# A two-layer decoder trunk on one core: the first head pair's weights made ahead of the first head's chain, and low parts moved behind the last one

## The chip, the cores and the metric

The kernel runs on one core of a Trainium2 chip. The metric is device time in microseconds (us) of one execution. A core has TensorE (PE, matmuls), VectorE (DVE), ScalarE (ACT), GpSimd (POOL) and SyncE (SP, which issues most DMAs), each with its own queue of instructions in program order; they wait for each other by semaphores.

## The reference

Two layers on a sequence of 1024 rows of width 1024, all in float32. The change touches the first layer's mixer, its output projection, and the start of its FFN.

```
def hgrn2_mixer(h, w_in, lower_bound, g_norm_w, w_out):
    q, f, i, g = jnp.split(h @ w_in, 4, axis=-1)          # 8 heads of 128 each
    fg = lb + (1.0 - lb) * jax.nn.sigmoid(heads(f))
    o = hgrn2_chunkwise(jax.nn.silu(heads(q)), 1.0 - fg, heads(i), jnp.log(fg))
    o = o * lax.rsqrt(jnp.mean(jnp.square(o), -1, keepdims=True) + RMS_EPS)
    o = o * g_norm_w * jax.nn.silu(heads(g))
    return o.reshape(B, S, D) @ w_out
...
h = layer_norm(ALPHA * h + mix, ln_mix_g[0], ln_mix_b[0])
ff = conv_ffn(h, ...)              # up-projection, causal conv of width 3, silu(a) * b, down-projection
h = layer_norm(ALPHA * h + ff, ...)
# then the shared K and V, and a layer with windowed attention and another FFN
```

hgrn2_chunkwise is a gated linear recurrence: a state of 128x128 per head that decays by fg and takes up k and v; in chunks it is a product of decayed scores, plus the carried state.

## The kernel before

**Precision.** Every large matmul is three: an operand is split into a high part (a cast on ScalarE to fp32r, line L249, L1285 or L868) and a low part (source minus high part, helper low_part, L197, on VectorE or POOL), and hi*hi, hi*lo and lo*hi are added in PSUM (helper mm3, lines L222, L223 and L224). T holds x transposed and split; HL is a ring of split weight blocks; raw0 to raw2 are the landing places of loaded weights (rx in the FFN), each loaded again when its last reader is done.

**Projections of the heads.** The weights of head pairs are multiplied by a scheme of seven products on block sums (Strassen's). Its products are numbered 1 to 7; a line of (pair m, product p) is worked through in order. Block sums of x stand in Y0, Y1 and a part of T: xf and xs are the sources, s1 is the tile VG of the "minus first" head, and sums_of_x and last_sums make them (L845 to L848, L868). Block sums of weights are the jobs "a" and "b" (L1305 to L1309): on POOL for pair 0, on VectorE for later ones. job_next makes a sum or a low part, cast_next a cast.

**The chain of a head (recur).** After fg, qs and kp of a head are there, VectorE runs products of decays in levels: L1116 to L1124 form the first, then update(1) to update(6), each L1105, L1107, L1110; between them TensorE makes scores into psax (L228), which masked copies (L1048, L1069) put into Ab and A. update(3) of the first head waits for kd scores. At the end stand the state's products (VG,kd and VG,A) and L1194, L1196. Each head's values and gates lie in VG (L750 to L759), its output is scaled by a square root from POOL (ss, L1223 and L1224) into og.

**What sets the order.** The part up to the first output rows stands in manual_schedule: each engine's order is the order of the code. Generators are stepped by an object od that keeps a modelled time for TensorE (od.t) and VectorE (od.v); a step says when it may come (od.behind), and od.fill is called in the gaps to lay weight jobs. So a cost in the code (od.vec) moves instructions. Outside manual_schedule the framework's scheduler sets the order of all engines.

**The tail.** After the last product, finished heads' outputs come back from memory (hod, L1440) and are split into T (move); out_split splits the four weight blocks of hgrn_w_out. out_pass (L1508) multiplies them for the first four blocks of 128 rows, with the last head missing; when that is done, out_part adds it, L380 adds the residual, and L263 to L283 are the LayerNorm, whose scale and shift are loaded as HL and rx (L414, L415). ffn's class Up takes rows transposed (L232), and its first product reads TX, the block sums of split rows; tiles of pool hp must be done with where TX is placed over them.

```
        VG = {-1: hp.tile([P, 2, S], F32, name="VG", bufs=2)}
        VG[0] = hp.tile([P, 2, S], F32, name="VG", bufs=2)
        ...
        with tc.manual_schedule(engines={EN.PE, EN.SP, EN.Activation, EN.DVE, EN.Pool}):
            pair_load(0, 0)
            od.fill, od.hook, od.room = lay, hook, 0.5
            first_qf(w0)
            pair_load(0, 1)
```

## Time and profile before

| | |
|---|---|
| time, three runs | 2133.52 us median (2132.39 to 2134.44) |
| profiled execution | 2132.9 us, span 2131.1 us |
| granted TensorE clock, mean | 0.996 |
| busy | TensorE 2093.3 us (98%), VectorE 1777.7 us (83%), ScalarE 968.5 us (45%), POOL 205.1 us (10%) |
| DMA | 286.81 MB, mean 135 GB/s |

A row of the timeline is: start in us, duration, engine, line, operation, output<-inputs, shape and count, and in brackets the idle time before it and who ended it. A row of the waits is: engine, tile and line that waited, for whom, then total us, times, and the longest. A row of a stretch of the span is: from:to, length, then busy us and instructions of PE, PEld (weight loads), DVE, ACT and POOL, the granted clock, the share of DMA and its GB/s. Lines after the change are a few higher: L1116 becomes L1125, L1105 becomes L1114, L1048 becomes L1057, L1305 becomes L1315 and so on.

### The profile page before, as it was taken

Reading aid. Unit: us, or ns where it says so; the run is one execution under the profiler, and the core shown is the slowest. Engines: PE = TensorE matmul, PEld = TensorE weight load, DVE = VectorE, ACT = ScalarE, POOL = GpSimd, SP = SyncE. Lnnn points to the kernel's source line nnn. Section 1 sums busy time; section 2 is a strip of 40 time slices with the busy share of each in tenths; the row PEclk is TensorE's granted clock in tenths of the full one; section 3 lists DMA queues with packets and bytes.
Section 4 is the critical chain, followed back from the end, with each engine's and each line's share of the span. In section 5 each row is a group of like instructions: output and inputs, shape, how many; then the busy total and the mean of one; then the engine's idle time right before and its main releaser. Section 6 shows DMA issues by size and latency. Waiting matters only on the chain. (4 is left out here: it accounts for less than half of the span.)

```text
span 2131.1 us, 31572 instructions
## 1 busy us (share of the span) xinstructions
PE 2093.3 (98%) x12303; PEld 1743.4 (82%) x12303; DVE 1777.7 (83%) x2408; ACT 968.5 (45%) x1562; POOL 205.1 (10%) x226
## 2 busy tenths in 40 slices
PE   9899999998999999999999999999999999999998
PEld 8688888887878888888888888888888888888886
DVE  6777777758999998887987758969999999978976
ACT  6455555542444444444433356743544444444430
POOL 2200000000110000100001113321010000000002
PEclk9999999999999999999999999999999999999999
DMA  4011111153238666627854511042266776449662
GB/s 152 21 51 52 54 59 57 55 179 99 89 101 196 160 168 160 164 97 260 300 185 157 172 26 46 23 149 89 81 172 173 176 170 156 129 146 332 224 206 99
DMA packets 239822, 286.81 MB, mean 135 GB/s; under 512 B 30216, under 2 KB 160440, under 8 KB 239416
## 3 DMA queue, kind: packets, MB, share of 16 engines
q1 hardware_dynamic: 223360, 238.26, 34.4%
q0 software_dynamic: 15456, 46.16, 10.9%
q8 instruction: 97, 1.59, 0.3%
q10 hardware_dynamic: 856, 0.37, 0.1%
q14 instruction: 53, 0.43, 0.1%
HBM read 241.72 MB, written 89.15 MB: 155 GB/s over the span
## 5 line engine op out<-in xcount | busy, mean ns | idle before, releaser
L222 PE MATMUL psmm<-T,HL 128*128 128x512 f32 x768 | 303.4, 395 | 0.7 <-ACT qs L1364 0.7
L224 PE MATMUL psmm<-T,HL 128*128 128x512 f32 x768 | 299.6, 390 | 3.0 <-DVE HL L197 3.0
L223 PE MATMUL psmm<-T,HL 128*128 128x512 f32 x768 | 299.1, 390 | 0.9 <-DVE T L197 0.9
L527 DVE SCALAR_TENSOR_TENSOR Y<-Y,cwt,Y 128x1023 f32<-128x1023 f32 (+1 forms) x176 | 225.3, 1282 | 49.0 <-ACT Y L525 47.5
L249 ACT CAST HL<-rx 128x1024 fp32r<-128x1024 f32 (+1 forms) x151 | 151.1, 1007 | 163.7 <-DMA rx<-in_ffn_w_in_dram 32.2
L197 DVE TENSOR_TENSOR HL<-rx,HL 128x1024 fp32r<-128x1024 f32 (+1 forms) x151 | 176.6, 1176 | 18.6 <-ACT HL L249 18.3
L224 PEld LDWEIGHTS psmm<-T,HL 128*128 128x128 f32 x768 | 144.2, 188 | 34.2 <-DVE HL L197 3.9
L223 PEld LDWEIGHTS psmm<-T,HL 128*128 128x128 f32 x768 | 144.4, 188 | 30.0 <-DVE T L197 1.3
L222 PEld LDWEIGHTS psmm<-T,HL 128*128 128x128 f32 x768 | 144.1, 188 | 30.1 <-ACT qs L1364 1.1
L525 ACT ACTIVATE Y<-Y,cwt 128x1024 f32<-128x1024 f32 x88 | 108.8, 1237 | 93.3 <-DVE Y L514 82.8
L222 PE MATMUL psax<-T,HL 128*128 128x512 f32 x352 | 137.3, 390 | 0.0
L224 PE MATMUL psax<-T,HL 128*128 128x512 f32 x352 | 137.0, 389 | 0.0
L223 PE MATMUL psax<-T,HL 128*128 128x512 f32 x352 | 136.9, 389 | 0.0
L197 DVE TENSOR_TENSOR HL<-raw,HL 128x512 fp32r<-128x512 f32 (+1 forms) x121 | 93.7, 798 | 45.7 <-ACT HL L1285 35.9
L271 POOL TENSOR_TENSOR rs<-rs,nhalf 128x1 f32<-128x1 f32 x32 | 45.0, 1406 | 738.1 <-DVE rs L270 738.1
L249 ACT CAST HT<-rx 128x1024 fp32r<-128x1024 f32 (+1 forms) x37 | 35.5, 960 | 135.9 <-DVE rx L481 62.9
L222 PE MATMUL psmm<-HL 128*128 128x512 f32 x220 | 86.8, 395 | 5.4 <-ACT qs L1364 5.4
L224 PE MATMUL psmm<-HL 128*128 128x512 f32 x220 | 86.2, 392 | 0.0
L223 PE MATMUL psmm<-HL 128*128 128x512 f32 x220 | 86.1, 391 | 0.0
L249 ACT CAST HL<-Y 128x1024 fp32r<-128x1024 f32 (+1 forms) x32 | 28.6, 894 | 109.3 <-DVE Y L481 44.5
L222 PEld LDWEIGHTS psax<-T,HL 128*128 128x128 f32 x352 | 66.2, 188 | 13.7
L224 PEld LDWEIGHTS psax<-T,HL 128*128 128x128 f32 x352 | 66.0, 188 | 13.7
(397 smaller groups left out, 5414.3 us busy)
## 6 DMA issues: line engine op xcount, KB each, us to landing
rx<-in_ffn_w_in_dram SPq DMA_DIRECT2D x136, 256.0 KB
rx<-gd SPq DMA_DIRECT2D x118, 256.0 KB
bsd<-in_ffn_w_out_dram POOLq DMA_DIRECT2D x36, 768.0 KB, 8.3
gd<-Y SPq DMA_DIRECT2D x44, 512.0 KB
raw<-in_hgrn_w_in_dram SPq DMA_DIRECT2D x30, 512.0 KB
rx<-in_ffn_w_out_dram SPq DMA_DIRECT2D x54, 256.0 KB
R<-bsd SPq DMA_DIRECT2D x44, 256.0 KB
Y<-in_ffn_w_in_dram SPq DMA_DIRECT2D x40, 256.0 KB
```

Source lines behind the costliest of these rows:

```text
L197: make = lambda e: e.tensor_tensor(lo, src, hi.bitcast(F32), op=ALU.subtract)
L222: nc.tensor.matmul(ps, st(0), mv(0), start=start, stop=False, skip_group_check=onto)
L223: nc.tensor.matmul(ps, st(0), mv(1), start=False, stop=False, skip_group_check=onto)
L224: nc.tensor.matmul(ps, st(1), mv(0), start=False, stop=stop, skip_group_check=onto)
L249: nc.scalar.copy(hi, src)
L271: nc.gpsimd.tensor_tensor(rs, rs, nhalf, op=ALU.pow)
L525: nc.scalar.activation(c, u, AF.Identity, bias=cwt[:, l, 3, ci:ci + 1], scale=cwt[:, l, 2, ci:ci + 1])
L527: nc.vector.scalar_tensor_tensor(c[:, sh:], u[:, :S - sh], cwt[:, l, 2 - sh, ci:ci + 1], c[:, sh:], op0=ALU.mult, op1=ALU.add)
```

## The change

Five things change. The first pair's second weights are loaded earlier in the program, and ensure(1) and ensure(3) force four of its blocks ahead of the first head's chain. The pair's sums and the low parts of x's last sums go from POOL to VectorE, the latter by a step that is placed by od.behind. VG has two named places with og between them, and Up's TX becomes TX and T2. Low parts of the output weights and of moved heads become lists (out_lows, moved_lows) that lay takes, the second only after the last head's update(6). The output passes run hi by hi for all four row blocks first. And manual_schedule ends ahead of the last out_part.

```diff
-            self.TX = pool.tile([P, 3, 2, 4, 512], F32R, name="TX")
+            self.TX = pool.tile([P, 2, 2, 4, 512], F32R, name="TX")
+            self.T2 = pool.tile([P, 2, 4, 512], F32R, name="T2")
...
-        for name, copies in (("fg", 1), ("qs", 1), ("kp", 2), ("kd", 1), ("tot", 1), ("St", 1), ("qp", 1), ("A", 1), ("og", 1)):
+        for name, copies in (("fg", 1), ("qs", 1), ("kp", 2), ("kd", 1), ("tot", 1), ("St", 1), ("qp", 1), ("A", 1)):
             hp.tile([P, S], F32, name=name, bufs=copies)
-        VG = {-1: hp.tile([P, 2, S], F32, name="VG", bufs=2)}
-        VG[0] = hp.tile([P, 2, S], F32, name="VG", bufs=2)
+        def values_and_gates(h):
+            return hp.tile([P, 2, S], F32, name=f"VG{h % 2}")
+        VG = {0: values_and_gates(0)}
+        hp.tile([P, S], F32, name="og")
+        VG[-1] = values_and_gates(-1)
...
                 nc.scalar.copy(t[:, 0], src)
-                low_part(t[:, 1], src, t[:, 0], nc.gpsimd)
-                yield 0.8
+                yield od.behind(0.0, 1.0)
+                low_part(t[:, 1], src, t[:, 0], None)
+                od.vec(0.7)
+                yield 0.1
...
                 proj_T(weights["f"], half, ps)
+                opened[0] = 2 * half
...
             update(6)
+            if h == NH - 1:
+                through.append(1)
...
-                make = nc.vector.tensor_tensor if m else nc.gpsimd.tensor_tensor
                 if p == "a":
-                    make(b12, b22, b12, op=sub)
-                    make(b11, b12, b11, op=add)
+                    tt(b12, b22, b12, op=sub)
+                    tt(b11, b12, b11, op=add)
...
-        later_dve = []
+        out_lows, moved_lows, through = [], [], []
         def lay():
-            if later_dve and later_dve[0][0] <= od.t:
-                later_dve.pop(0)[1]()
+            if job_next():
                 return True
-            return job_next()
+            lows = out_lows or (moved_lows if through else [])
+            if lows and lows[0][0] <= od.t:
+                lows.pop(0)[1]()
+                return True
+            return False
...
             pair_load(0, 0)
+            pair_load(0, 1)
             od.fill, od.hook, od.room = lay, hook, 0.5
             first_qf(w0)
-            pair_load(0, 1)
             pair_load(1, 0)
+            ensure(1)
             opened[0] = 4
             od.finish(fourth)
+            ensure(3)
...
             for tb in range(4):
                 begun.append(psmm())
                 out_pass(begun[tb], tb, 0, 0, range(KC - 2), start=True)
+            lay_all(out_lows)
+            for tb in range(4):
                 out_pass(begun[tb], tb, 0, 1, range(KC - 2))
             od.finish(moved)
             for tb in range(4):
                 out_pass(begun[tb], tb, 0, 0, [KC - 2])
                 out_pass(begun[tb], tb, 0, 1, [KC - 2])
+            lay_all(moved_lows)
+            for tb in range(4):
                 out_pass(begun[tb], tb, 1, 0, range(KC - 1))
...
-            od.fill = od.hook = None
+        od.fill = od.hook = None
...
```

**Where it moves instructions.** On VectorE at the start, between the last low parts of x's sums (Y_309 is Y0) and the first operation of the first head's chain, L1116 (St<-qs,kp). Before:

```order
L197 TENSOR_TENSOR Y_309<-kp,Y_309 128x4x128
L197 TENSOR_TENSOR HL<-kd,HL 128x4x128
L197 TENSOR_TENSOR Y_309<-kd,Y_309 128x4x128
L1116 TENSOR_TENSOR St<-qs,kp 128x1024
L1117 TENSOR_TENSOR qp<-qs,fg 128x1024
```

After, where Y_463 is Y1, raw_113 and raw_114 are the landing places raw1 and raw2, and the chain begins at L1125:

```order
L197 TENSOR_TENSOR Y_309<-kd,Y_309 128x4x128
L197 TENSOR_TENSOR Y_463<-St,Y_463 128x4x128
L197 TENSOR_TENSOR HL<-raw_113,HL 128x512
L1315 TENSOR_TENSOR raw_114<-raw_114 128x512
L1316 TENSOR_TENSOR raw_113<-raw_114,raw_113 128x512
L197 TENSOR_TENSOR Y_463<-qp,Y_463 128x4x128
L197 TENSOR_TENSOR HL<-raw_113,HL 128x512
L197 TENSOR_TENSOR Y_463<-tot,Y_463 128x4x128
L197 TENSOR_TENSOR Y_463<-og,Y_463 128x4x128
L197 TENSOR_TENSOR HL<-raw_113,HL 128x512
L1318 TENSOR_TENSOR raw_113<-raw_113 128x512
L1319 TENSOR_TENSOR raw_113<-raw_114,raw_113 128x512
```

A further HL low part follows, and then L1125: twelve operations came in ahead of the chain.

On VectorE further down in the first head's chain, from its update(4) (the L1114, L1116 and L1119 of 128x32x16) to update(5), after the change; VG_125 is VG1, the sums s1 of x, and T<-VG_125 are three of its four low parts, which POOL made before:

```order
L1114 TENSOR_TENSOR qp<-qp,tot 128x32x16
L1116 TENSOR_TENSOR kp<-kp,tot 128x32x16
L1119 TENSOR_TENSOR tot<-tot 128x32
L1078 COPY_PREDICATED Ab<-msk,psax 128x16x8
L1057 COPY_PREDICATED Ab<-msk,psax 128x64x2 x2
L197 TENSOR_TENSOR T<-VG_125,T 128x4x128 x3
L197 TENSOR_TENSOR HL<-raw_113,HL 128x512
L197 TENSOR_TENSOR HL<-raw_112,HL 128x512
L1114 TENSOR_TENSOR qp<-qp,tot 128x16x32
```

The same place on TensorE after the change, from the kd scores to the first products of p5, which read the T that those low parts write (the rows of T,HL):

```order
L228 MATMUL psax<-kd 32x16 x32
L228 MATMUL psax<-qp,kp 32x32 x16
L222 MATMUL psmm<-HL 128x512
L223 MATMUL psmm<-HL 128x512
L224 MATMUL psmm<-HL 128x512
L222 MATMUL psmm<-HL 128x512
L223 MATMUL psmm<-HL 128x512
L224 MATMUL psmm<-HL 128x512
L222 MATMUL psmm<-T,HL 128x512
L223 MATMUL psmm<-T,HL 128x512
```

Six matmuls stand between the scores and p5; the low parts that p5 reads stand behind update(3) and update(4).

On VectorE in the last head's chain before, from the end of update(4) to update(5):

```order
L1048 COPY_PREDICATED Ab<-msk,psax 128x64x2 x2
L197 TENSOR_TENSOR T<-fg,T 128x2x512
L197 TENSOR_TENSOR T<-VG,T 128x512
L197 TENSOR_TENSOR T<-qs,T 128x2x512
L197 TENSOR_TENSOR T<-kp,T 128x2x512
L197 TENSOR_TENSOR T<-Y_4183,T 128x2x512 x2
L197 TENSOR_TENSOR HL<-raw_114,HL 128x1024
L1105 TENSOR_TENSOR qp<-qp,tot 128x16x32
```

And after, from update(5)'s start past update(6):

```order
L1114 TENSOR_TENSOR qp<-qp,tot 128x16x32
L1116 TENSOR_TENSOR kp<-kp,tot 128x16x32
L1119 TENSOR_TENSOR tot<-tot 128x16
L1078 COPY_PREDICATED Ab<-msk,psax 128x8x16
L1114 TENSOR_TENSOR qp<-qp,tot 128x8x64
L1116 TENSOR_TENSOR kp<-kp,tot 128x8x64
L1119 TENSOR_TENSOR tot<-tot 128x8
L197 TENSOR_TENSOR HL<-raw_113,HL 128x1024
L197 TENSOR_TENSOR HL<-raw_114,HL 128x1024
L197 TENSOR_TENSOR T<-fg,T 128x2x512
L197 TENSOR_TENSOR T<-VG_3508,T 128x512
L197 TENSOR_TENSOR T<-qs,T 128x2x512
```

The low parts of moved heads (T) and of the output weights (HL<-raw) went from between the two updates to behind the last one.

## The prediction

> **What bounds the kernel now.** I read the page's first part, then the waits of TensorE (PE), then a table of stretches of the span.

> ```profile
> span 2131.1 us, 31572 instructions
> PE 2093.3 (98%) x12303; PEld 1743.4 (82%) x12303; DVE 1777.7 (83%) x2408; ACT 968.5 (45%) x1562; POOL 205.1 (10%) x226
> ```

> ```profile
> PE psmm L224 <- DVE HL L197: 6.5, 3, 3.5
> PE psmm L222 <- ACT qs L1364: 6.0, 2, 5.4
> PE psmm L232 <- DVE Y L283: 5.3, 1, 5.3
> PE psmm L222 <- ACT fg L1362: 2.2, 1, 2.2
> PE psmm L222 <- ACT T L249: 1.0, 1, 1.0
> PE psax L232 <- DVE og L1226: 1.0, 1, 1.0
> ```

> ```profile
> 60.00:100.00 40.00, 29.62 (x395) 23.18 (x394) 27.10 (x49) 19.70 (x38) 10.30 (x7) 0.96 0.10 27
> 100.00:430.00 330.00, 325.79 (x3196) 271.22 (x3195) 250.06 (x445) 184.81 (x402) 16.80 (x14) 1.00 0.18 55
> 430.00:530.00 100.00, 92.20 (x693) 75.49 (x692) 68.60 (x109) 35.86 (x65) 6.32 (x5) 0.97 0.42 143
> 530.00:640.00 110.00, 106.53 (x486) 88.00 (x486) 103.96 (x137) 48.94 (x65) 14.28 (x9) 0.98 0.29 94
> 640.00:2120.00 1480.00, 1479.87 (x7214) 1234.55 (x7214) 1283.02 (x1604) 645.35 (x941) 142.26 (x171) 1.00 0.55 158
> ```

> PE is idle 37.8 us in all (2131.1 - 2093.3), and the table says where: 10.4 us in 60 to 100 (the first head's chain), 4.2 in 100 to 430, 7.8 in 430 to 530 (output projection and first LayerNorm), 3.5 in 530 to 640, none from 640 to 2120; the 11.8 left over lie before 60 and behind 2120, where nothing changes. No matmul is removed, so there is a gain only in the first four rows, and what the granted clock lost there (0.96, 0.97 and 0.98 in the eighth figure). The four longest waits are single events, which I looked at in time order.

> ```profile
> 66.27 0.50 PE L224 MATMUL psmm<-T,HL 128*128 128x512 f32 x1 [2.81 <-DVE HL L197]
> 76.32 0.50 PE L222 MATMUL psmm<-Y,HL 128*128 128x512 f32 x1 [2.21 <-ACT fg L1362]
> 88.82 0.80 PE L222 MATMUL psmm<-HL 128*128 128x512 f32 x1 [5.35 <-ACT qs L1364]
> 89.41 0.63 PE L223 MATMUL psmm<-HL 128*128 128x512 f32 x1
> 89.84 0.63 PE L224 MATMUL psmm<-HL 128*128 128x512 f32 x1
> 93.71 0.47 PE L222 MATMUL psmm<-HL 128*128 128x512 f32 x1
> 96.09 0.39 PE L223 MATMUL psmm<-T,HL 128*128 128x512 f32 x1
> 96.32 0.39 PE L224 MATMUL psmm<-T,HL 128*128 128x512 f32 x1
> ```

> A 128x512 matmul starts every 0.23 us (96.09, 96.32). After the 5.35 us wait they start every 0.43 us (89.41, 89.84), until 93.71: the granted clock is halved for 4.9 us. Six matmuls lie in that time at 0.20 us extra each, 1.2 us; if all of it were lost by half it would be 2.4; I take 1.7. After the two shorter waits the clock stays.

> **Part 1, the start: first pair's weights ahead of the chain, on VectorE.** What goes away: POOL's share. In this row POOL waited 11 us for its turn, and PE waited behind it for the first low part:

> ```profile
> 66.45 1.52 POOL L1306 TENSOR_TENSOR raw<-raw,raw 128x512 f32<-128x512 f32 x1 [11.07 <-DVE HL L197]
> ```

> With all of the pair's blocks made ahead, the waits of 2.81, 2.21 and 5.35 and the clock's 1.7, with 0.1 for each of three restarts, are open to be won: 12.4 us. That is the bound of gain. Against it stands what now waits instead.

> ```profile
> 48.82 0.68 DVE L197 TENSOR_TENSOR Y<-kd,Y 128x512 fp32r<-128x512 f32 x1
> 52.43 1.80 DVE L1116 TENSOR_TENSOR St<-qs,kp 128x1024 f32<-128x1024 f32 x1 [2.93 <-ACT qs L1033]
> 59.03 1.29 DVE L1124 TENSOR_TENSOR kd<-kp,qp 128x512 f32<-128x512 f32 x2
> 420.61 1.22 DVE L1116 TENSOR_TENSOR St<-qs,kp 128x1024 f32<-128x1024 f32 x1
> 425.55 1.28 DVE L1124 TENSOR_TENSOR kd<-kp,qp 128x512 f32<-128x512 f32 x2
> 440.34 0.69 DVE L1105 TENSOR_TENSOR qp<-qp,tot 128x512 f32<-128x512 f32 x1 [2.72 <-PE psax L228]
> 445.23 1.25 DVE L197 TENSOR_TENSOR T<-fg,T 128x1024 fp32r<-128x1024 f32 x1
> ```

> (a) Between Y<-kd (ends 49.5) and L1116 the order now has 12 more VectorE operations of 128x512 (four low parts of Y1, four of HL, four sums). Two such operations start 0.60 us apart (1.29 for the two at 59.03), so 7.2 us, and some 0.8 for two sums that read the one ahead and a cast of ScalarE: L1116 starts near 57.5 instead of 52.43. Of these 5.1 us, 2.9 were idle time. From there the chain takes 7.8 us before (52.43 to the end of 59.03's pair, 60.2) but 6.1 for the last head, where POOL is quiet (420.61 to 426.75), so the first head's kd is ready near 63.6, 3.4 us late. The first weight product waits for a sum that stands right behind kd; it began at 62.82 and now at about 64.0: 1.2 us lost. Bounds: 0, if the cast is not waited for, and 3.4.

> (b) The product of Y0 still waits for ScalarE's copy into fg, which now stands behind a cast of VG1 and four casts of HL; my walk gives 1.4 us, between 0 and the 2.21 of its row today.

> (c) A wait that was not there. Three of the four low parts T<-VG1 now stand on VectorE behind the first head's update(3), the masked copies and update(4), and update(3) needs the kd scores. PE has only 6 products between those scores and product p5, which reads T<-VG1. From the end of the scores VectorE needs 0.1 + 4.9 us (the last head's 440.34 to 445.23, same rows) + three low parts of 0.6 = 6.9; PE has 6 x 0.23 = 1.4 of work, and one matmul more when the cast is done: 5.2 us of idle. Bounds: 0, if the low parts run sooner than I read it, and 5.35, the like wait before, whose place it takes. I take 5.2, since order and durations both come from rows. A wait of that length cost the clock before, so 1.7 again, and 0.1 for each of three restarts.

> Sum for the start: 12.4 - (1.2 + 1.4 + 5.2 + 1.7 + 0.3) = 2.6 us gained, with ends of 12.4 gained and, if every new wait took its upper end (3.4 + 2.2 + 5.35 + 2.4 + 0.3 = 13.7), 1.3 lost. POOL has no other work there. SyncE's order in the start is unchanged; the load of the next pair's weights is freed by a low part that stands behind (c), some 3 us later than now, and PE, 2.6 ahead, has then 5.6 us less slack for it; this price I cannot bound better than 0 to 5.6, and take 0, since 36 matmuls stand between (c) and the state's products.

> **Part 2, the heads between.** Heads 1 to 6 keep their steps; a few rows change places. 4.2 us of idle in 330 is all there is to win; I take 0, within 1 us.

> **Part 3, the tail.** Low parts of moved heads and of the output weights leave the last head's chain:

> ```profile
> 451.52 1.22 DVE L197 TENSOR_TENSOR HL<-raw,HL 128x1024 fp32r<-128x1024 f32 x1
> 467.72 0.29 DVE L1194 COPY St<-psax 128x128 f32<-128x128 f32 x1 [10.46 <-PE psax L228]
> 487.44 2.94 ACT L249 CAST TX<-rx 128x1024 fp32r<-128x1024 f32 x3 [0.57 <-DVE T L197]
> 498.87 1.22 DVE L197 TENSOR_TENSOR TX<-rx,TX 128x1024 fp32r<-128x1024 f32 x1
> 514.94 0.34 SPq L415 DMA_DIRECT2D rx<-in_ln_mix_b_dram  x1
> 518.55 2.46 DVE L283 SCALAR_TENSOR_TENSOR Y<-Y,rs,rx 128x1024 f32<-128x1024 f32 x2
> 519.88 1.97 PE L232 MATMUL psmm<-ident,Y 128*128 128x128 f32 x8 [5.33 <-DVE Y L283]
> 522.07 0.63 PE L223 MATMUL psmm<-TX,T 128*128 128x512 f32 x1
> ```

> From 445.23 to 452.7 VectorE made low parts while update(5) waited: 7.5 us. Now update(5) follows update(4) but for one masked-copy group and one low part. PE had products to run meanwhile, so most of the 7.5 is no gain: what falls is 1.0 and 1.0 of the waits rows (og, T L249), 2.0 us. Its bounds are 0 and 2.2 (a restart of 0.1 each). The low parts that moved lie behind update(6) now, where VectorE stood idle for 10.46 us; they fit in there with 7.2 us, and if that cover failed the lo-by-hi passes, last in PE's order, would wait up to that long. On SyncE the loads of moved heads now stand ahead of the last loads of x; I price that at nothing, since TX's first casts wait for VectorE and not for a load (487.44), and at 4 us if x came late for them.

> Next, the LayerNorm. PE ends the first-layer products at 514.55 and waits 5.33 us for L283, which waits for the load at 514.94, issued when HT and HL low parts free its place. TX now has its own place and its casts follow the last T<-VG cast; the four TX low parts come about 3.5 us sooner, then the load, then L283, so the transposes start near 516.2 instead of 519.88: 3.7 us gained in all, 2.0 by the above and 1.7 by a shorter wait (3.6 us). Bounds: 2.0, if only PE gets ahead and VectorE does not, and 7.3, if the wait goes. Product order (hi by hi first) changes no number of matmuls.

> After that wait the matmuls ran at 0.63 each (522.07), half clock, 2 to 3 us of loss. I keep that loss at 3.6 us, since the wait of 3.47 in the FFN lost its clock too (0.63 until 627.15):

> ```profile
> 622.50 1.22 DVE L197 TENSOR_TENSOR HL<-Y,HL 128x1024 fp32r<-128x1024 f32 x1
> 623.78 0.50 PE L224 MATMUL psmm<-TX,HL 128*128 128x512 f32 x1 [3.47 <-DVE HL L197]
> 627.15 0.63 PE L224 MATMUL psmm<-TX,HL 128*128 128x512 f32 x1
> ```

> [...]

> **Part 4, the first FFN.**

> The manual order ends earlier now, and from there VectorE's order is another: the low part at 622.50 and the one ahead of it stand before three evacuations. The wait of 3.47 and 1.4 us of half clock behind it (seven matmuls at 0.20) go: 4.9. But six more VectorE operations stand ahead of two evacuations that PE waits for about 10 us earlier, and VectorE is busy 104 of 110 us here, so up to 5 us come back. I take 3.0 gained; bounds -1 and 4.9.

> **Sum:** 2.6 + 0 + 3.7 + 3.0 = 9.3 us, from the profiled execution's 2132.9 to 2123.6. That run lies 0.6 below the median of the three (2133.52), so 2124.2; I say 2124.

> **Rivals.**
> 1. *The new wait (c) does not bite*, since VectorE reaches the T<-VG1 low parts in time. Against it stands the order alone, timed by rows of another head. Then 5.2 + 1.7 more: 2117. Chance 0.12.
> 2. *The half clock after the LayerNorm's 3.6 us wait is escaped.* For it: waits of 2.81 and 2.21 kept the clock; against it, 3.47 lost it. 2.6 less: 2121.5. Chance 0.13.
> 3. *Nothing arrives.* The start only exchanges waits (its lower end), VectorE in the FFN, 95% busy, takes back the tail's gain: 2.6 and 3.0 of the sum go, and part of 3.7. About 2131, within 0.2% (4.3 us, about what a measurement tells from no change). Chance 0.18.
> 4. *Slower.* The stretch of heads 1 to 6 has rows that change places too. Should each of its six heads and the last now wait 2 us at its update(3), as the first does for 5, 14 us are lost: 2124 + 14 = 2138. It decides from 1.9 us a head (9.3 + 4.3 over 7). Against it: 4.2 us of idle in 330 today, 0.6 a head. Chance 0.08.

> My forecast, with sizes within 4 us of the sum, has 0.49. Faster by over 0.2%: 0.49 + 0.12 + 0.13 = 0.74; within: 0.18; slower: 0.08. The range reaches to rival 1 with the FFN's better bound and part of (a) and (b), 2113, and above past rival 3, 2133; about 0.1 lies on either side. Forecast alone: 2120 to 2128.

> **What would show it.** Right: no POOL row but the square roots before 430; PE's waits at 66, 76 and 89 gone, with waits of about 1 us at 64 and 70, and one of about 5 us near 83 to 88 for T<-VG1 (ACT or DVE), half clock behind it; the first kd state products at about 100; LayerNorm transposes with a wait of 3 to 4 us; no HL wait near 615. Wrong: a wait in a stretch I gave as unchanged (100 to 430, or 530 to 640), a wait (c) that is gone, or transposes of the LayerNorm with as long a wait as before.

## The result, and the profile after

The changed kernel takes 2127.11 us (median of 7 runs, 2124.68 to 2128.41) against 2133.52 (7 runs, 2132.32 to 2134.44): a ratio of 0.997, 95% interval 0.9958 to 0.9981. It is faster by 0.3%. The profiled execution of after took 2124.68 us, the fastest of the seven, 2.4 below their median. Each experiment's ratio is to runs of before that were taken beside it (medians 2132.82 to 2133.81), and a run of e4 of 6086.06 us is left out.

The profile's first part and, from the waits of TensorE, the two longest (us in total, times, longest):

```profile
span 2122.8 us, 31567 instructions
PE 2093.4 (99%) x12303; PEld 1740.8 (82%) x12303; DVE 1777.7 (84%) x2420; ACT 965.2 (45%) x1562; POOL 187.2 (9%) x214
```

```profile
PE psmm L222 <- ACT T L874: 3.6, 1, 3.6
PE psmm L222 <- DVE VG L1390: 2.8, 1, 2.8
```

PE's busy time is the same (2093.4 against 2093.3), so the 8.3 us of span are idle time, 37.8 us before and 29.4 now. The waits of 6.5, 6.0 and 5.3 us are gone from the head of the list. Two new ones stand there: 3.6 us for a block sum of x (cast at L874, low part at L197) and 2.8 us for a weight product's evacuation (L1390). The stretches, with the same bounds as before:

```profile
60.00:100.00 40.00, 33.24 (x389) 25.22 (x388) 24.92 (x50) 17.31 (x34) 0.00 (x0) 0.87 0.10 27
100.00:430.00 330.00, 323.81 (x3192) 268.77 (x3191) 248.12 (x445) 184.73 (x402) 16.84 (x14) 1.00 0.18 54
430.00:530.00 100.00, 96.99 (x732) 79.85 (x731) 74.86 (x119) 36.90 (x67) 7.77 (x6) 1.00 0.44 145
530.00:640.00 110.00, 109.06 (x499) 89.59 (x497) 102.81 (x132) 51.22 (x69) 14.40 (x9) 1.00 0.34 104
```

From 60 to 100 PE is busier by 3.6 us (33.24 against 29.62), but the granted clock fell from 0.96 to 0.87. The clock was 0.50 for 10.2 of these 40 us (71.33 to 74.74 and 81.57 to 88.40), before for 3.4 (88.65 to 92.06). By the mean clock c I count (1 - c) of the stretch as lost, idle time in it included: 5.2 us now, 1.6 before. So the clock takes back about the 3.6 us that the waits gave. Part of that is chance in before's profile: in those of e2, e6 and e7, whose order is the same there, this row has 0.87 too. From 100 to 430 PE is idle 2.0 us longer. The gain stands in the last two rows: 4.8 us more of busy time from 430 to 530, 2.5 from 530 to 640, both at a clock of 1.00 instead of 0.97 and 0.98. The events behind these rows, from PE's timeline:

```profile
63.19 0.50 PE L222 MATMUL psmm<-T,HL 128*128 128x512 f32 x1 [0.41 <-DVE VG L758]
70.80 0.50 PE L222 MATMUL psmm<-Y,HL 128*128 128x512 f32 x1 [1.85 <-ACT fg L1378]
71.38 0.63 PE L224 MATMUL psmm<-Y,HL 128*128 128x512 f32 x1
81.53 0.79 PE L222 MATMUL psmm<-T,HL 128*128 128x512 f32 x1 [3.64 <-ACT T L874]
83.18 0.79 PE L223 MATMUL psmm<-T,HL 128*128 128x512 f32 x1 [0.86 <-DVE T L197]
188.25 0.47 PE L222 MATMUL psmm<-T,HL 128*128 128x512 f32 x1 [2.81 <-DVE VG L1390]
413.58 1.72 PE L228 MATMUL psax<-VG,kd 128*128 128x128 f32 x14
516.71 1.09 PE L232 MATMUL psmm<-ident,Y 128*128 128x128 f32 x8 [1.99 <-DVE Y L283]
517.89 0.39 PE L223 MATMUL psmm<-TX,T 128*128 128x512 f32 x1
```

The waits in the start now cost 6.8 us instead of 10.4, with half clock behind two of them: four matmuls of 128x512 from 71.38 on, and thirteen from 81.53 to 88.04, most at 0.63 us each where it is 0.39 at full clock. Where the seventh head's state products begin (413.58), the changed kernel is 2.0 us late: before they began at

```profile
411.58 1.72 PE L228 MATMUL psax<-VG,kd 128*128 128x128 f32 x14
```

At the LayerNorm's transposes it leads by 3.2 us (516.71 against 519.88), and no half clock follows them (0.39 at 517.89). So by these two profiles 2.0 us were lost up to 413, and 10.3 won behind it. The 2.0 are within chance: e2, e6 and e7 reach the same products at 412.92 to 413.70.

### The profile page after: what moved, and what is told of

Its sections match the earlier page's. It is cut to its first block, busy times and chain, and to the rows that moved or that the text cites. A ratio compares the mean times of both kernels' runs of the same rounds, so it can differ in the third digit from the quotient of the medians.

```text
span 2122.8 us, 31567 instructions
## 1 busy us (share of the span) xinstructions
PE 2093.4 (99%) x12303; PEld 1740.8 (82%) x12303; DVE 1777.7 (84%) x2420; ACT 965.2 (45%) x1562; POOL 187.2 (9%) x214
## 5 line engine op out<-in xcount | busy, mean ns | idle before, releaser
L222 PE MATMUL psmm<-T,HL 128*128 128x512 f32 x816 | 323.1, 396 | 6.9 <-ACT T L874 3.6
L223 PE MATMUL psmm<-T,HL 128*128 128x512 f32 x816 | 319.0, 391 | 1.7 <-DVE T L197 1.7
L224 PE MATMUL psmm<-T,HL 128*128 128x512 f32 x816 | 319.2, 391 | 0.3 <-DVE HL L197 0.2
L249 ACT CAST HL<-rx 128x1024 fp32r<-128x1024 f32 (+1 forms) x151 | 150.8, 1005 | 149.8 <-DMA rx<-in_ffn_w_in_dram 33.1
L197 DVE TENSOR_TENSOR HL<-rx,HL 128x1024 fp32r<-128x1024 f32 (+1 forms) x151 | 180.1, 1198 | 14.9 <-ACT HL L249 14.5
L222 PEld LDWEIGHTS psmm<-T,HL 128*128 128x128 f32 x816 | 153.8, 188 | 38.9 <-ACT T L874 4.1
L224 PEld LDWEIGHTS psmm<-T,HL 128*128 128x128 f32 x816 | 153.7, 188 | 33.6 <-DVE HL L197 1.2
L223 PEld LDWEIGHTS psmm<-T,HL 128*128 128x128 f32 x816 | 153.9, 189 | 33.3 <-DVE T L197 2.7
L222 PE MATMUL psax<-T,HL 128*128 128x512 f32 x392 | 153.2, 391 | 1.3 <-DVE Y L513 0.9
L224 PE MATMUL psax<-T,HL 128*128 128x512 f32 x392 | 152.6, 389 | 0.0
L223 PE MATMUL psax<-T,HL 128*128 128x512 f32 x392 | 152.5, 389 | 0.0
L197 DVE TENSOR_TENSOR HL<-raw,HL 128x512 fp32r<-128x512 f32 (+1 forms) x121 | 92.7, 788 | 43.2 <-ACT HL L1296 33.5
L249 ACT CAST HT<-rx 128x1024 fp32r<-128x1024 f32 (+1 forms) x37 | 35.5, 960 | 146.1 <-DVE rx L482 62.0
L222 PEld LDWEIGHTS psax<-T,HL 128*128 128x128 f32 x392 | 73.6, 188 | 17.6 <-DVE Y L513 1.3
L222 PE MATMUL psmm<-HL 128*128 128x512 f32 x220 | 86.5, 393 | 0.0
L224 PEld LDWEIGHTS psax<-T,HL 128*128 128x128 f32 x392 | 73.6, 188 | 15.4
L223 PEld LDWEIGHTS psax<-T,HL 128*128 128x128 f32 x392 | 73.6, 188 | 15.0
L224 PE MATMUL psmm<-HL 128*128 128x512 f32 x220 | 85.7, 390 | 0.0
L223 PE MATMUL psmm<-HL 128*128 128x512 f32 x220 | 85.6, 389 | 0.0
```

The costliest lines, as they stand in the source:

```text
L197: make = lambda e: e.tensor_tensor(lo, src, hi.bitcast(F32), op=ALU.subtract)
L222: nc.tensor.matmul(ps, st(0), mv(0), start=start, stop=False, skip_group_check=onto)
L223: nc.tensor.matmul(ps, st(0), mv(1), start=False, stop=False, skip_group_check=onto)
L224: nc.tensor.matmul(ps, st(1), mv(0), start=False, stop=stop, skip_group_check=onto)
L249: nc.scalar.copy(hi, src)
```

## The experiments

My theory after this: the gain belongs to the tail alone, and the start, which is the larger part of the code, gives back what it takes. Rivals: the start gains as predicted and the tail less; the new tile places (VG, TX and T2) carry the tail; SyncE's order of loads carries it.

**e1, the start alone.** Before, with only the start's part of the diff, the pair's sums and x's last low parts on VectorE included:

```
 pair_load(0, 0)
+pair_load(0, 1)
...
+ensure(1)
...
+ensure(3)
...
```

> Only the start's part of the change (second weights loaded earlier, four blocks forced ahead of the first chain, sums and x's low parts on VectorE); the tail is that of before. My theory, from the trace after: the start wins 0.8 us up to the first head's state products, and then one wait of 2.8 us for L1390 near 188 is new, because the changed costs moved a pair of weight sums behind update(3) of a later head; so this part by itself is a loss of about 2 us: some 2135.5 us, the last head's VG,kd 2 us later than before (468), the wait at 188 there. Rival A: the start is a gain and the 2.8 us wait comes from the tail's part: then 2 to 3 us below before, no wait at 188. Rival B: the loss is taken back by the LayerNorm's wait: no change within 1 us.

2134.73 us (11 runs), ratio 1.0005 (0.9996 to 1.0014): no gain. Its PE timeline has after's waits:

```profile
79.67 0.49 PE L222 MATMUL psmm<-T,HL 128*128 128x512 f32 x1 [3.63 <-ACT T L868]
413.34 1.72 PE L228 MATMUL psax<-VG,kd 128*128 128x128 f32 x14
521.71 1.97 PE L232 MATMUL psmm<-ident,Y 128*128 128x128 f32 x8 [5.43 <-DVE Y L283]
```

The seventh head's products begin at 413.34, 1.8 us behind before's profile, and the LayerNorm's wait is before's. The start's new waits take back what its old ones gave.

**e2, the tail alone.** Before, with only the tail's part (lists of low parts, tile places, passes, end of the manual order):

```
+lows = out_lows or (moved_lows if through else [])
...
-    od.finish(normed)
+od.finish(normed)
```

> Only the tail's part of the change (places of VG, og, TX and T2, the lists of low parts, hi by hi passes first, the end of the manual order); the start is that of before, up to the last head's chain. My theory: everything that the whole change won comes from here, about 10 us (2.0 of idle ahead of the first FFN matmuls, 3.3 of the LayerNorm's wait, 2.5 of its half clock, 2.5 to 4 in the FFN): 2123 to 2124 us, about 2 to 3 below the whole change. Rival: the tail's gain needs the start (its shift of PE against VectorE); then it is 2127 or more, with a LayerNorm wait over 3 us.

2125.54 us (5 runs), ratio 0.9963 (0.9951 to 0.9976): the whole gain. By the medians it is 7.3 below before, where the change is 6.4; the intervals overlap, so this 1 us is not shown, and the 10 us that I expected did not come. The start is not needed for the gain.

**e4, old tile places.** After, with VG in two buffers, og in its old place and TX of three parts:

```
-self.TX = pool.tile([P, 2, 2, 4, 512], F32R, name="TX")
-self.T2 = pool.tile([P, 2, 4, 512], F32R, name="T2")
+self.TX = pool.tile([P, 3, 2, 4, 512], F32R, name="TX")
```

> The changed kernel with the tile places of before: two rotating VG, og with the others, one TX of three parts. The order of all VectorE operations is that of the changed kernel. If the place of TX is what lets the LayerNorm start sooner, its wait comes back from 2.0 to about 4 to 5 us with half clock behind it, and the time is 4 to 6 us over the changed kernel (about 2132). If the order alone does it, the wait stays 2.0 us and the time is 2127.

2125.51 us (4 runs), ratio 0.9965 (0.995 to 0.998). The gain stays, so the places are not worth the 4 to 6 us that my expectation allowed them. The LayerNorm's wait is 1.0 us longer than after's, and six matmuls at half clock (0.60 to 0.78 us) lie behind it; the median does not show them:

```profile
516.04 1.54 PE L232 MATMUL psmm<-ident,Y 128*128 128x128 f32 x8 [2.97 <-DVE Y L283]
```

**e5, the manual order ends where it did.** After, with the last two output parts back under manual_schedule:

```
-        od.fill = od.hook = None
-        ps = psax()
...
+            od.fill = od.hook = None
+            ps = psax()
```

> The changed kernel with manual_schedule ending where it did before (behind the last output parts). The order of VectorE from the LayerNorm through the first FFN products is then near that of before. If the end of the manual order is what removed the 3.47 us wait for HL in the FFN, the wait is back near 615 with half clock, and the time is some 3 to 5 us over the changed kernel (2130 to 2132). If the earlier TX low parts did it, no such wait and 2127.

2133.43 us (10 runs), ratio 1.0004 (0.9995 to 1.0013). Six lines of indentation take back all of the gain that the medians show, more than the 3 to 5 us that I expected. Both of the tail's waits are back, with half clock behind them:

```profile
522.13 1.95 PE L232 MATMUL psmm<-ident,Y 128*128 128x128 f32 x8 [4.88 <-DVE Y L283]
524.30 0.63 PE L223 MATMUL psmm<-TX,T 128*128 128x512 f32 x1
624.70 0.79 PE L224 MATMUL psmm<-TX,HL 128*128 128x512 f32 x1 [3.16 <-DVE HL L197]
```

What this edit moves can be read on VectorE and ScalarE, where the last head's gated values (L1251) become the last part of T. The last row of each block is a stretch from the first of these products to L283, the LayerNorm's last step. In e5 the code's order goes piece by piece, product, cast, low part:

```profile
484.44 0.48 DVE L1251 SCALAR_TENSOR_TENSOR VG<-psax,par,VG 128x256 f32<-128x256 f32 x1 [6.69 <-PE psax L232]
485.39 0.43 DVE L197 TENSOR_TENSOR T<-VG,T 128x256 fp32r<-128x256 f32 x1 [0.47 <-ACT T L249]
494.77 2.34 DVE L197 TENSOR_TENSOR TX<-rx,TX 128x1024 fp32r<-128x1024 f32 x2
484.44:520.79 36.35, 32.50 (x141) 25.85 (x139) 31.46 (x49) 10.36 (x13) 3.04 (x2) 1.00 0.29 89
```

In after the scheduler takes three products together, then three casts, then three low parts:

```profile
481.94 1.27 DVE L1251 SCALAR_TENSOR_TENSOR VG<-psax,par,VG 128x256 f32<-128x256 f32 x3 [6.68 <-PE psax L232]
482.45 1.19 ACT L249 CAST T<-VG 128x256 fp32r<-128x256 f32 x3 [10.46 <-DVE VG L1251]
483.12 1.08 DVE L197 TENSOR_TENSOR T<-VG,T 128x256 fp32r<-128x256 f32 x3
490.22 2.35 DVE L197 TENSOR_TENSOR TX<-rx,TX 128x1024 fp32r<-128x1024 f32 x2
481.94:515.38 33.44, 32.47 (x141) 25.94 (x139) 30.14 (x47) 10.33 (x13) 2.55 (x2) 1.00 0.34 101
```

From the first product to TX's first low parts it is 10.33 us in e5 and 8.28 in after, and to L283 36.35 and 33.44. The 2.9 us are the difference of the two LayerNorm waits, 4.88 - 1.99. VectorE is busy 31.46 us of this stretch in e5 and 30.14 in after: 1.3 us of work less stands ahead of L283, one residual sum (L380) and one operation of statistics (L263), and 1.6 us of idle time is gone (4.89 against 3.30). The wait for a cast between pieces is a small part of that: up to TX's first low parts VectorE idles 0.67 us in e5 and not at all in after.

**e6, only that edit.** Before, with nothing changed but the end of manual_schedule, moved ahead of the last output parts:

> The kernel before with one edit alone: manual_schedule ends ahead of the last output parts, as in the change. From the LayerNorm on its order of VectorE and SyncE is that of the changed kernel; everything ahead is that of before. My theory: this one edit carries the change's gain: LayerNorm wait from 5.3 to about 2.5 us without half clock, no HL wait near 620; 5 to 8 us under before (2125 to 2128), of the 8 us that the whole tail part won. Rival: the moved low parts and the new order of the output passes are needed to be early enough: LayerNorm wait over 4 us, gain under 3 us.

2127.37 us (6 runs), ratio 0.9968 (0.9956 to 0.998): the same as the whole change, within the intervals. By the profiles, PE and POOL work through the same order as in before. ScalarE's order first differs at 525, behind the LayerNorm's transposes, and VectorE's at the T<-VG low part at 482.66 of before. Its LayerNorm wait fell from 5.33 to 2.93, though TX stands in its old place and the low parts of moved heads still stand in the chain:

```profile
483.78 1.27 DVE L1240 SCALAR_TENSOR_TENSOR VG<-psax,par,VG 128x256 f32<-128x256 f32 x3 [3.83 <-PE psax L232]
492.06 2.34 DVE L197 TENSOR_TENSOR TX<-rx,TX 128x1024 fp32r<-128x1024 f32 x2
519.48 1.09 PE L232 MATMUL psmm<-ident,Y 128*128 128x128 f32 x8 [2.93 <-DVE Y L283]
```

It is 8.28 us again from the first product to TX's low parts. Eight matmuls ran at half clock (0.63 us) behind the 2.93 us, where I expected none. In the FFN the wait of 3.47 is gone; the largest there are 0.99 and 1.27 us.

The rest of the tail's edits are worth something, though. From the seventh head's state products to the first product that reads TX (L222, psmm<-TX,T) it is 84.6 to 84.7 us in all seven profiles with the new lists and passes, e4 with its old places among them, and 86.4 to 86.5 in the four without (before, e1, e6 and e7). These 1.8 us are less than the intervals of the ratios can tell.

**e7, SyncE's order of loads.** The edit also let the FFN's weight loads go ahead of the load of the LayerNorm's scale (HL from gd). Here before gets that order by the code:

```
-ff.row_loads()
 ff.weights(1)
+ff.row_loads()
```

> The kernel before with two code lines swapped: ff.weights(1) ahead of ff.row_loads(). On SyncE two weight loads (L470) then stand ahead of the load of the LayerNorm's scale (HL<-gd, L414), which waits for PE to free its place; in the end part VectorE keeps its manual order. If the loads queued behind that wait are what made the LayerNorm late, its wait falls from 5.3 to 2 to 3 us and the half clock goes: 4 to 6 us under before, with the HL wait near 620 still there. If VectorE's order at the end of the manual part did it, the LayerNorm's wait stays over 4 us and the gain is under 2 us.

2132.12 us (11 runs), ratio 0.9993 (0.9984 to 1.0001). By the ratio that is 1.5 us, and its interval reaches from none to 3.4. Both waits stay, the LayerNorm's shorter by 0.9 us than before's 5.33:

```profile
520.70 1.90 PE L232 MATMUL psmm<-ident,Y 128*128 128x128 f32 x8 [4.42 <-DVE Y L283]
623.48 0.80 PE L224 MATMUL psmm<-TX,HL 128*128 128x512 f32 x1 [3.31 <-DVE HL L197]
```

SyncE's order up to the LayerNorm is now that of e6, whose wait is another 1.5 us shorter (2.93). So the order of loads carries the lesser part at most, and for the rest of the LayerNorm's wait only VectorE's order is left. No edit made that order by hand. How much of the gain is the LayerNorm's and how much the FFN's was not separated by an edit: the same end of the manual order sets both.

**e8, low parts ahead of update(3).** The start's two new waits have one cause. On VectorE of after, the T<-VG1 low parts stand behind update(3) and update(4) of the first head, and two heads later a weight sum (L1318, L1319) and a product's evacuation do:

```profile
76.38 0.69 DVE L1114 TENSOR_TENSOR qp<-qp,tot 128x512 f32<-128x512 f32 x1 [4.31 <-PE psax L228]
81.22 1.91 DVE L197 TENSOR_TENSOR T<-VG,T 128x512 fp32r<-128x512 f32 x3
179.83 0.69 DVE L1114 TENSOR_TENSOR qp<-qp,tot 128x512 f32<-128x512 f32 x1 [1.73 <-PE psax L228]
184.70 0.71 DVE L1318 TENSOR_TENSOR raw<-raw 128x512 f32<-128x512 f32 x1
187.43 0.68 DVE L1390 TENSOR_TENSOR VG<-VG,psmm 128x512 f32<-128x512 f32 x1
```

Before, that evacuation stood just ahead of update(3):

```profile
183.62 0.68 DVE L1374 TENSOR_TENSOR VG<-VG,psmm 128x512 f32<-128x512 f32 x1
184.22 0.68 DVE L1105 TENSOR_TENSOR qp<-qp,tot 128x512 f32<-128x512 f32 x1
```

VectorE idles 4.31 us at 76.38 with the low parts queued behind. e8 steps them as soon as their cast is due, and opens the later weight jobs two products later:

```
-    yield od.behind(0.0, 1.0)
+    yield 0.6 if not part else od.behind(0.0, 1.0)
...
-opened[0] = len(line)
...
+    if n == 2:
+        opened[0] = len(line)
```

> The changed kernel with T<-VG1's casts and low parts laid at once (0.6 us of model time instead of od.behind), so all four stand ahead of the first head's update(3), and the next pair's casts held back until product 2, so that the copy into fg is not behind them. By the theory of the new wait for T<-VG1 (4.5 us with half clock behind it) and of the moved sums (2.8 us near 188), both waits go, the fg wait falls from 1.85 to under 1, and the time is 8 to 11 us under the changed kernel: 2116 to 2119. Rival: the chain's products simply wait elsewhere (VectorE is late at update(3) by the 2 us of low parts): 2122 to 2125.

2115.28 us (4 runs), ratio 0.9914 (0.99 to 0.9928). This is the lowest median, 18.5 us below before and, across two sets of runs, 11.8 below after.

```profile
60.00:100.00 40.00, 37.08 (x440) 29.95 (x438) 30.51 (x62) 24.00 (x45) 0.00 (x0) 1.00 0.10 28
```

```profile
69.86 0.50 PE L222 MATMUL psmm<-Y,HL 128*128 128x512 f32 x1 [0.83 <-ACT fg L1378]
402.38 1.72 PE L228 MATMUL psax<-VG,kd 128*128 128x128 f32 x14
```

The two edits were not separated. The seventh head's products begin 11.2 us earlier than in after. That is 3.8 us of waits in the start (6.76 down to 2.92), 5.2 of clock (0.87 to 1.00 over 40 us) and 2.0 of idle time from 100 to 430, where the 2.8 of the wait at 188 go and 0.9 of others (L1194) come: 11.0 together.

**e3, the same low parts on POOL.** After, with x's last low parts on POOL as before:

```
-    yield od.behind(0.0, 1.0)
-    low_part(t[:, 1], src, t[:, 0], None)
-    od.vec(0.7)
...
+    low_part(t[:, 1], src, t[:, 0], nc.gpsimd)
...
```

> The changed kernel with the low parts of x's last sums (Y1 and T<-VG1, eight operations) on POOL again; weight sums stay on VectorE. Theory: the 2.8 us wait near 188 goes (VectorE's order there is that of before), the T<-VG1 wait shrinks from 4.5 to about 2.5 us, as the last cast still stands behind the chain's copies; VectorE's chain runs slower beside POOL (1.80 instead of 1.22 us for L1125). 3 to 5 us under the changed kernel, 2122 to 2124. Rival: VectorE beside POOL loses what the wait gains: 2126 or more.

2115.87 us (4 runs), ratio 0.9922 (0.9908 to 0.9935): as good as e8, and 6 to 8 us better than I expected. That the wait at 188 goes without the od.vec costs of these low parts was expected. What was better is the start: the product behind T<-VG1 waits 1.2 us (2.5 expected, 4.5 in after), and the only half clock there is 3.4 us behind the wait of 2.0, where after has 10.2. The first product of VectorE's chain (L1123, 57.92) takes 1.22 us, as in after, where 1.80 was expected. PE's longest waits in the start:

```profile
PE psmm L222 <- DVE VG L758: 2.0, 1, 2.0
PE psmm L223 <- POOL T L197: 1.2, 1, 1.2
```

e3 differs from e2 by the weights made ahead, with their sums on VectorE, and has a ratio of 0.9922 against 0.9963. So these were the half of the start's change that won; x's low parts on VectorE, where od placed them, were the half that cost.

**e11, do the two add up?** e8 with the manual order ended as before:

> The version with the low parts ahead of update(3) (2115.3 us, ratio 0.991), with the manual order of the tail ended again behind the last two output parts, as the kernel before has it. If start and tail add up, as the theory has it: the tail's 6.3 us (the difference that this edit made to the changed kernel, 2133.4 against 2127.1) come back, so about 2121.6, ratio 0.9945, with a LayerNorm wait of 4.4 to 5.4 us with half clock behind it, and the FFN's wait of some 3.2 us for an HL low part at about 615. Rival: the tail's gain was not in the order but in how late PE came to the tail; PE now comes there some 12 us earlier than in the changed kernel, so the waits would be longer still, and the time 2124 or more (LayerNorm wait above 6 us). Second rival: the start's gain is the whole of it and the manual order's end costs nothing once PE is early, 2115 to 2117.

2121.57 us (4 runs), ratio 0.9944 (0.9928 to 0.9961), as the theory has it (2121.6).

```profile
508.71 1.97 PE L232 MATMUL psmm<-ident,Y 128*128 128x128 f32 x8 [5.10 <-DVE Y L283]
611.84 0.80 PE L224 MATMUL psmm<-TX,HL 128*128 128x512 f32 x1 [3.76 <-DVE HL L197]
```

PE comes to the tail 11 us earlier than in after (402.46 at the seventh head's products), and the waits are as long as e5's or a little longer: the order sets them, not how late PE is; PE's order is the same in e8 and e11. 6.3 us come back, as in e5.

## Why the prediction was right, point by point

2124 was forecast and 2127.11 measured, inside 2113 to 2133 and on the side that had the most chance. Taken term by term, in the profiled execution (9.3 us forecast, 8.3 of span measured), two errors cancel.

- **The clock of before, as I read it.** I put the half clock behind the 5.35 us wait at 4.9 us, until 93.71. The granted clock of before is 0.50 from 88.65 to 92.06, 3.4 us. The 1.7 that I took is half of that, so the sum has the right number from a wrong length. The 0.1 for a restart is the 0.50 us of the first matmul behind a wait (66.27, 76.32) less the 0.39 of those at full clock (96.09).
- **(a), the sums ahead of the chain: right in mechanism.** The first weight product waited 0.41 us (1.2 forecast). The first product of the chain began at 56.59 instead of 57.5 and took 1.22 us with POOL idle, where before's row at 52.43 has 1.80 beside work of POOL (51.85 to 55.38):

```profile
56.59 1.22 DVE L1125 TENSOR_TENSOR St<-qs,kp 128x1024 f32<-128x1024 f32 x1
```

- **(b), the copy into fg: 1.85 us (1.4 forecast).** The half clock behind it (71.38) was not in the sum.
- **(c), the new wait: it came, as the longest one.** Rival 1 is refuted. It was 4.5 us in two pieces (5.2 forecast), with thirteen matmuls at half clock, 2.6 us at 0.20 each instead of 1.7. I had the place wrong: "update(3) needs the kd scores", I wrote, but it went at 76.38, when the scores ahead of those were done, and the wait stands at 81.5. The kd scores come at 89.69, so the TensorE rows shown with the change are of a later place. The rest of the reckoning holds at the right place: six matmuls stand between those earlier scores and the wait, and VectorE takes 4.84 us from update(3) to the low parts (4.9 reckoned).
- **Sum of the start: mis-sized.** 2.6 was forecast; at the first head's state products after leads before's profile by 0.8 us (they begin at 102.59 and 96.54, with thirty products of 0.23 us more ahead of them in after). The lost term is the clock: I charged one half-clock stretch of 1.7, and after shows two, of 3.4 and 6.8 us. As e2, e6 and e7 have two of these lengths in before's order too, and after leads them by 2.3 to 2.6 us there, the difference to the forecast is the luck of before's profile as much as an error.
- **Part 2, the heads: the step that failed.** "Heads 1 to 6 keep their steps" missed the 2.81 us at 188. The costs of the sums and low parts (od.vec) moved a weight sum and an evacuation behind update(3) of a later head. Rival 4 named that place with 2 us a head; it happened once. e3, without the low parts' costs, has no such wait. Start and heads together lost 2.0 us up to 413 where 2.6 won was forecast; e1's ratio of 1.0005 (0.9996 to 1.0014) says that they give nothing.
- **Part 3, the tail: right in size, half wrong in cause.** From 411.58 and 413.58 to the transposes the change wins 5.2 us (3.7 forecast): 3.3 by the shorter wait, 1.8 ahead of it, where 2.0 was forecast. The 1.8 are what the new lists and passes give, as forecast: wherever the lists are, the wait of 1.0 us for og is gone and that for T (L249) is 0.3 us instead of 1.0. The shorter wait I ascribed to TX's own place and the thinner chain; e4 and e6 show that neither is needed for most of it (2.97 and 2.93 us against 5.33).
- **Rival 2, half clock escaped: it happened.** The 0.39 at 517.89 shows the clock kept; from the transposes to the FFN's first products another 2.4 us are won. The 2.6 of that rival is an estimate of mine that no run shows; the 2.4 stand in its place. The clock was kept behind a wait of 1.99 us, though, not 3.6; after waits of 2.83 to 2.97 us in e4, e6 and e8 six to eight matmuls ran at half clock (0.63 us).
- **Part 4, the FFN: 2.7 us won (3.0 forecast),** from a lead of 5.6 us at a product of HT (L222, psax<-TX,HT, 595.09 against 600.65) to 8.3 at the end. The wait of 3.47 went with its clock; 0.90 and 0.44 us are what came back.
- **Rival 3, nothing arrives,** is true of the start alone (e1), not of the tail.

4.6 us too many for start and heads, 1.5 too few for the tail, 2.4 too few for the clock: the number came out because of these signs, which is luck. What was sound was the list of places; what I did not see is that the end of manual_schedule carries most of it.

## What to carry to other kernels

- Where an order is partly by hand and partly the scheduler's, the place where the one ends is a parameter to be tried by itself. Here it alone gave 6.4 us (e6): with two operations fewer ahead of L283 and less idle time between, VectorE was done 2.5 to 2.9 us sooner.
- Work moved to the engine of a serial chain must stand ahead of the chain's waits, not behind them: here low parts behind update(3), and the jobs that their costs displaced, took some 11 us with the half clock behind their waits (e8 and e3).
- A planner's cost for one instruction moves others. Look for the row that moved two heads later before you price a stretch at nothing.

## What the runs showed of the hardware

The granted clock of before is 0.50 from 88.65 to 92.06, from 518.73 to 525.56 and from 624.54 to 627.96, that of after from 71.33 to 74.74 and from 81.57 to 88.40. Each of these five stretches is 3.41 or 6.83 us long; both profiles have another at the end of the span (from 2126.41 and 2119.33 on). The wait at 66 in before lies in two stretches of 3.41 us, with 1.30 and 1.51 us of it, and the clock stays (the third row):

```profile
61.34:64.76 3.42, 2.12 (x12) 1.49 (x10) 2.49 (x6) 2.02 (x5) 0.00 (x0) 1.00 0.00 0
64.76:68.17 3.41, 1.90 (x11) 1.32 (x15) 2.06 (x5) 0.59 (x2) 1.52 (x1) 1.00 0.02 5
68.17:71.58 3.41, 3.41 (x157) 2.85 (x158) 1.76 (x2) 1.49 (x3) 2.36 (x2) 1.00 0.02 5
```

In e6 all 2.76 us lie in one, and the next one runs at half clock:

```profile
63.47:66.88 3.41, 0.65 (x3) 0.30 (x2) 3.15 (x7) 0.92 (x3) 0.16 (x1) 1.00 0.00 0
66.88:70.29 3.41, 3.41 (x15) 2.04 (x17) 0.90 (x2) 1.66 (x3) 2.16 (x2) 0.50 0.02 5
```

In after PE was idle for 1.85 us from 67.92 to 71.33, and half clock followed. Of the 2.81 us at 188, 1.94 lie from 183.97 to 187.38 and 0.87 behind, and the clock stayed at 1.00. So a wait of 1.85 to 3.07 us came out either way in these profiles; the cause was not shown. If PE has work throughout, half clock costs half of its stretch, 1.7 us of 3.41 or 3.4 of 6.83 (an estimate; matmuls of 128x512 start 0.43 us apart at half clock, 0.23 at full).

**The clock is part of the spread.** The seven runs of after have spans from 2122.8 us, at a mean granted clock of 0.997, to 2126.5 at 0.995. A clock lower by 0.002 over this span is 4.2 us of work; the spans differ by 3.7. One run does not fit, 2126.1 us at 0.997, so the clock is not all of it.
